# Two weight loads ahead of the second modulation group, convolution vectors moved up, and another order of passes in the first unit of a block

## The chip, the cores and the metric

The kernel runs on one core of a Trainium2 chip. The metric is device time of one execution in microseconds (us). Matmuls run on TensorE (PE in the profile; PEld is its weight load), elementwise work on VectorE (DVE), ScalarE (ACT) and GpSimd (POOL). Nearly all DMAs are issued by SyncE (SP), in the order of its program; a few small ones by ACT.

## What is computed

One layer of a decoder with T = 256 positions and D = 2048 channels, in float32:

```python
mod = silu(c) @ w_ada + b_ada            # shift, scale, gate for each of the two sub-layers
h   = rms_norm(x, g_mix_norm) * (1 + scale1) + shift1
p   = h @ w_in                           # columns: GLA k, q, v, gates; attention q, k, v
o   = concat(diff_attention(...), gla_chunked(...))
x   = x + gate1 * (o @ w_o)
h2  = rms_norm(x, g_ffn_norm) * (1 + scale2) + shift2
g, u = split(h2 @ w_up)
x   = x + gate2 * ((gelu(causal_dwconv(g, w_conv, b_conv)) * u) @ w_down)
out = rms_norm(x, g_final)
```

## The kernel before

**Units of weights.** Each weight matrix comes in units of 512 KB, two rows of 128 by 512 columns. `load_unit` (L110) has SP load a unit into `raw` (L120), lets ACT copy it into `wh`, rounded to the matmul's type (L123), and DVE subtract that from `raw` to give the low part `wl` (L124). The inputs (`hT`, `mixT`, `h2T`) are kept as a high and a low part too. A product is three matmuls: `wh` by high, `wh` by low, `wl` by high. `b_block` (L128, transposed output) and `a_block` (L159) run them. `wh` and `wl` have three buffers each, `raw` has six.

**The modulation vectors.** `w_ada` is multiplied in the background, by `ada_gen` (L219). Its loads `raw_a` (L240, 512 KB; L243 for the first group, in halves) use the same six buffers and the same queue of SP as the weights. The first of a group's 16 steps is an ACT multiplication into `acc` (L263), the other 15 are DVE multiply-adds (L265), each on top of the one before. Then PE sums over the partitions into `ps_mod` (L233), and DVE makes the columns `s` and `sh` of them (L278 to L281). Below, the 16 loads of the second group are called k0 to k15, and the first weight units w1, w2 and so on. How many background steps run per weight unit is a rate: `load_unit` adds `rate[0]` to a credit and takes one step for each whole credit. For the input projection `R_K` (L33) gives a rate for each of four input groups. `drain` runs a generator until a named step is done.

**Stages.** The input projection goes over four groups of 2, 4, 4 and 6 input tiles (loop at L747). In each group nine blocks of output columns are accumulated: the two lead blocks gk and gq half by half, then gv0, gv1, gg0, gg1, dq0, dk0, dv0. Group 0 needs the first modulation group, input group 1 the second. `norm_T` (L291) makes two input tiles: DVE scales by the row norm (L297), ACT applies `s` and `sh`. With gran = 1 (only the very first pair, of `hT` and of `h2T`) ACT writes the high part (L302) and the value `xv` itself (L304) tile by tile; otherwise the value (L304) and then both high parts at once (L306). DVE subtracts for the low part (L307).

Then come three later blocks, attention and GLA, and the output projection (`wo_part`): its first two column blocks in three parts of 4, 2 and 2 units, between them the second half of the attention in the background. After the last part of these stands the load of the convolution vectors (L845 to L851): four times a small DMA on ACT's queue into `cst` (three buffers), a transpose on PE and a copy on ACT. The up projection (`ps_h`) follows, in groups of 4, 4 and 8 input tiles, then the down projection.

**The order of the work.** The order of the instructions on an engine is set by a scheduler of the framework, which goes by priorities and a timeline of its own. An edit in one place can so move instructions in others. Each engine carries out its list in order, and a DMA is issued when SP's list comes to it and its buffer is free.

Of the kernel before, what the change touches and what calls it, by code (L numbers as in the profile page):

```python
# [7 lines left out]
F32 = mybir.dt.float32  # L8
# [3 lines left out]
AF = mybir.ActivationFunctionType  # L12
ALU = mybir.AluOpType
AX = mybir.AxisListType

P = 128
# [9 lines left out]
FT = D_FF // P  # L26
# [5 lines left out]

R_K, R_LATER, R_WO, R_SP, R_UP = (2.2, 1.15, 1.3, 1.0), 0.5, 0.8, 0.9, 0.27  # L33

# [12 lines left out]
def tile_decoder_layer(  # L47
# [46 lines left out]
    def drain(name):  # L94
        while any(n == name for n, _ in bg):
            step()
# [3 lines left out]
    def slot(tag, shape, dtype, name, bufs):  # L100
# [5 lines left out]
        return stage.tile(shape, dtype, tag=tag, name=name, bufs=bufs)  # L106

    def load_unit(view, kt, c0):
        credit[0] += rate[0]
        while credit[0] >= 1.0:  # L110
# [16 lines left out]
    def b_block(ps, view, c0, kts, xt, first, last, done=None, tail=0):  # L127
# [5 lines left out]
        for gi, group in enumerate(groups):  # L133
            ws = [(kt, *load_unit(view, kt, c0)) for kt in group]
            seq = [(kt, h, l, j, m) for kt, h, l in ws for j in range(2) for m in range(4)]
            if len(group) > 1:
                seq.sort(key=lambda x: x[4] // 2)
            for kt, h, l, j, m in seq:
                k = kt + j
                ms = slice(m * P, (m + 1) * P)  # L140
                for i, (w, xx) in enumerate(((h, 0), (h, 1), (l, 0))):
                    PE.matmul(  # L142
                        ps[:, m * T:(m + 1) * T], w[:, j, ms], xt[k][:, xx, :],
# [147 lines left out]
    def norm_T(tmp, rst, s_col, sh_col, k0, name, gran):  # L291
# [3 lines left out]
        for j in range(0, 2, gran):  # L295
# [3 lines left out]
            for i in range(j, j + gran):  # L299
                k = k0 + i  # L300
                if gran == 1:
                    A.activation(res[:, 0, i], val[:, i], AF.Identity, scale=s_col[:, k:k + 1],  # L302
                                 bias=sh_col[:, k:k + 1])
                A.activation(val[:, i], val[:, i], AF.Identity, scale=s_col[:, k:k + 1], bias=sh_col[:, k:k + 1])  # L304
            if gran > 1:
# [441 lines left out]
    for g, kts in enumerate(KG):  # L747
        last = g == len(KG) - 1
        drain(f"norm{kts[0]}")
        rate[0] = R_K[g]  # L750
        if g == 1:
# [57 lines left out]


    drain("gt1")
    KO = list(range(8, 16)) + list(range(0, 8))
# [26 lines left out]
    for a, b in ((0, 8), (8, 12), (12, 16)):  # L839
        if b == KT:  # L840
            fdrain()
        for nb in range(2):
            wo_part(nb, po[nb], a, b)

    for j in range(4):  # L845
        cst = t1.tile([FT, P], F32, tag="w2", name="cst", bufs=3)
        src = w_conv[0, j] if j < 3 else b_conv[0]
        nc.scalar.dma_start(out=cst, in_=src.rearrange("(r p) -> r p", p=P))
        ps = pss.tile([P, 512], F32, tag="ms", name="ps_cv")
        PE.transpose(ps[:, 0:FT], cst, ident[0:FT, 0:FT])  # L850
        A.activation(nconv[:, j], ps[:, 0:FT], AF.Copy)  # L851
    for nb in range(2, 4):
# [177 lines left out]
```

## Time and profile before

| | |
|---|---|
| median of 3 runs | 1301.42 us (1301.13 to 1303.23) |
| the profiled execution | 1301.91 us |
| its span, first to last instruction | 1300.2 us |
| PE busy | 1239.3 us |
| DVE busy | 888.1 us |
| ACT busy | 702.3 us |
| read from HBM | 311 MB |

All times in the rows below are microseconds from the start of the span of the one profiled execution. A row of a timeline gives start, duration and engine; `x2` marks merged instructions. An engine with a q behind its name (SPq, ACTq) is the issue of a DMA. The square bracket names the idle time before an instruction and the instruction whose end released it. The granted clock (PEclk) is a share of TensorE's full speed: 1.00 is 2.4 GHz, 0.50 is 1.2 GHz.

### The profile page before, as it was taken

The page shows a single profiled execution, that of the slowest core. Times are in us where ns is not written, and L with a number is a line of the kernel's source. Part 1 is how long each engine was busy: PE and PEld are TensorE (multiplying, and loading weights), DVE is VectorE, ACT ScalarE, POOL GpSimd, SP SyncE. Part 2 cuts the span into 40 slices and gives each one's busy share as a digit, 9 for nine tenths or more (in the row PEclk, how much of TensorE's full clock was granted, in tenths as well). Part 3 has the DMA queues.
Part 4 walks back from the last instruction along what each step waited for, and adds up shares of the span by engine and source line. Part 5 has one row for each costly group of instructions (what it writes and reads, how often), then busy time and mean ns, then how long its engine had stood idle before and what let it go on. Part 6 is the DMA issues. An engine that isn't in the chain of part 4 may idle for free.

```text
span 1300.2 us, 21317 instructions
## 1 busy us (share of the span) xinstructions
PE 1239.3 (95%) x8492; PEld 1145.4 (88%) x8492; DVE 888.1 (68%) x1137; ACT 702.3 (54%) x913; POOL 38.3 (3%) x79
## 2 busy tenths in 40 slices
PE   4799999999999989899999999999999999999996
PEld 3588898888888889799999999999999988888885
DVE  5788888877667666777765777766667554545454
ACT  5377676854544434566776665744444543434343
POOL 3044000000000000000000000000000000000000
PEclk9899999999999989899999999999999999999999
DMA  8999999875477657699897777766677855555562
GB/s 301 321 346 336 353 336 324 266 236 179 146 232 243 196 170 227 231 360 341 294 336 224 228 225 223 235 215 194 203 233 234 274 168 194 193 194 194 181 208 82
DMA packets 159827, 314.57 MB, mean 242 GB/s; under 512 B 12046, under 2 KB 20942, under 8 KB 159727
## 3 DMA queue, kind: packets, MB, share of 16 engines
q1 hardware_dynamic: 155328, 307.28, 72.4%
q10 hardware_dynamic: 4398, 5.93, 1.3%
q8 instruction: 66, 1.08, 0.3%
q14 instruction: 35, 0.28, 0.1%
HBM read 311.07 MB, written 2.10 MB: 241 GB/s over the span
## 4 chain that ended last, share of the span: by engine, by line
PE 82%; DMA 8%; DVE 5%; ACT 2%; issue 2%; DVEq 0%; ACTq 0%
PE ps_h L142 39%; PE ps_d L176 18%; PE ps_mm L142 8%; PE ps_mm L176 6%; DMA raw_a<-in_w_ada_dram 5%; PE ps_o L142 5%; DVE acc L265 2%; DMA raw<-in_w_in_dram 2%; DVE wl L124 1%; PE ps_mod L233 1%; PE ps_s L590 1%; ACT wh L123 1%; PE ps_a L533 1%; DMA xtok<-in_x_dram 1%; DMA dlam<-in_diff_lambda_dram 1%
## 5 line engine op out<-in xcount | busy, mean ns | idle before, releaser
L124 DVE TENSOR_TENSOR wl<-raw,wh 128x1024 fp32r<-128x1024 f32 x339 | 413.9, 1223 | 220.2 <-ACT wh L123 218.9
L123 ACT ACTIVATE wh<-raw 128x1024 fp32r<-128x1024 f32 x339 | 357.6, 1057 | 372.1 <-PE ps_d L176 123.0
L142 PE MATMUL ps_h<-h2T,wh 128*128 128x256 f32 x2304 | 419.2, 284 | 4.7 <-ACT h2T L302 3.5
L142 PEld LDWEIGHTS ps_h<-h2T,wh 128*128 128x128 f32 x2304 | 360.7, 193 | 5.4 <-ACT h2T L302 3.9
L142 PE MATMUL ps_h<-h2T,wl 128*128 128x256 f32 x1152 | 326.7, 284 | 0.0
L265 DVE SCALAR_TENSOR_TENSOR acc<-raw_a,cols,acc 128x1024 f32<-128x1024 f32 (+1 forms) x180 | 216.3, 1202 | 89.5 <-DMA raw_a<-in_w_ada_dram 88.0
L142 PEld LDWEIGHTS ps_h<-h2T,wl 128*128 128x128 f32 x1152 | 221.7, 192 | 0.0
L176 PE MATMUL ps_d<-wh,act 128*128 128x512 f32 x704 | 217.4, 389 | 0.8 <-DVE dx L988 0.8
L176 PEld LDWEIGHTS ps_d<-wh,act 128*128 128x128 f32 x704 | 132.1, 188 | 29.3 <-DVE dx L988 1.2
L142 PE MATMUL ps_mm<-hT,wh 128*128 128x256 f32 x768 | 144.7, 289 | 7.2 <-ACT wh L123 6.3
L176 PE MATMUL ps_d<-wl,act 128*128 128x512 f32 x352 | 137.8, 391 | 0.0
L142 PEld LDWEIGHTS ps_mm<-hT,wh 128*128 128x128 f32 x768 | 122.5, 196 | 10.3 <-ACT wh L123 6.9
L176 PE MATMUL ps_mm<-wh,hT 128*128 128x512 f32 x384 | 123.9, 398 | 6.1 <-ACT wh L123 5.2
L142 PE MATMUL ps_mm<-hT,wl 128*128 128x256 f32 x384 | 110.8, 290 | 1.5 <-DVE wl L124 1.5
L142 PE MATMUL ps_o<-mixT,wh 128*128 128x256 f32 x512 | 97.3, 291 | 4.5 <-ACT mixT L475 2.6
L142 PE MATMUL ps_h<-h2T,late 128*128 128x256 f32 x768 | 97.4, 283 | 0.0
L142 PEld LDWEIGHTS ps_h<-h2T,late 128*128 128x128 f32 x768 | 94.4, 192 | 0.0
L176 PEld LDWEIGHTS ps_mm<-wh,hT 128*128 128x128 f32 x384 | 73.4, 192 | 22.9 <-ACT wh L123 6.2
L142 PEld LDWEIGHTS ps_o<-mixT,wh 128*128 128x128 f32 x512 | 82.2, 197 | 6.6 <-ACT mixT L475 3.2
L176 PE MATMUL ps_mm<-wl,hT 128*128 128x512 f32 x192 | 77.5, 404 | 2.5 <-DVE wl L124 2.5
L176 PEld LDWEIGHTS ps_d<-wl,act 128*128 128x128 f32 x352 | 66.1, 188 | 13.9 <-issue 0.5
L142 PEld LDWEIGHTS ps_mm<-hT,wl 128*128 128x128 f32 x384 | 74.8, 195 | 2.5 <-DVE wl L124 2.0
(247 smaller groups left out, 1125.2 us busy)
## 6 DMA issues: line engine op xcount, KB each, us to landing
raw_a<-in_w_ada_dram SPq DMA_DIRECT2D x162, 512.0 KB, 5.0
raw<-in_w_up_dram SPq DMA_DIRECT2D x143, 512.0 KB, 4.6
raw<-in_w_in_dram SPq DMA_DIRECT2D x96, 512.0 KB, 5.5
raw<-in_w_down_dram SPq DMA_DIRECT2D x88, 512.0 KB, 4.2
late<-in_w_up_dram SPq DMA_DIRECT2D x33, 512.0 KB, 4.8
raw<-in_w_o_dram SPq DMA_DIRECT2D x32, 512.0 KB, 4.7
raw_a<-in_w_ada_dram SPq DMA_DIRECT2D x32, 256.0 KB, 5.4
late<-in_w_ada_dram SPq DMA_DIRECT2D x14, 512.0 KB, 5.2
```

Of the source, the lines that this page charges most:

```text
L123: A.activation(h, raw, AF.Copy)
L124: V.tensor_tensor(l, raw, h, op=ALU.subtract)
L142: PE.matmul(ps[:, m * T:(m + 1) * T], w[:, j, ms], xt[k][:, xx, :], start=(first and k == kts[0] and m % 2 == 0 and i == 0), stop=(last an ...
L176: PE.matmul(ps[:, tb * 512:(tb + 1) * 512], xt[k][:, xx, tsl], w[:, j, :], start=(first and k == kts[0] and i == 0), stop=(last and k == k ...
L233: PE.matmul(ps[:, i:i + 1], src[:, i * P:(i + 1) * P], col, start=(not began and i == 0), stop=False, skip_group_check=True)
L265: pin(V.scalar_tensor_tensor(acc, raw[:, j], col, acc, op0=ALU.mult, op1=ALU.add))
L533: PE.matmul(pv[:, i, tb], lhs, rhs, start=True, stop=True)
L590: PE.matmul(pv, q[rs, hb * T + tb * P:hb * T + (tb + 1) * P], k[rs, hb * T:hb * T + n], start=False, stop=(tb == 1), skip_group_check=True)
```

## The change

It has four parts. The first weight units of the two lead blocks are requested right after the inputs of group 0 are drained, before the rate is set and so without any background step between them (`pre`); they are handed out when `load_unit` is asked for them. To take up for the two units without credit, the rate of group 0 is 2.7 for 2.2. In `norm_T` with gran = 1, DVE writes the value instead of ACT. In `b_block`, the first unit of a block that has more than one unit runs `wh` by high and `wl` by high for all its columns first, and `wh` by low last. The loads of the convolution vectors move from the end of the first two column blocks of the output projection to before it.

```diff
-R_K, R_LATER, R_WO, R_SP, R_UP = (2.2, 1.15, 1.3, 1.0), 0.5, 0.8, 0.9, 0.27
+R_K, R_LATER, R_WO, R_SP, R_UP = (2.7, 1.15, 1.3, 1.0), 0.5, 0.8, 0.9, 0.27
...
+    pre = {}
+
     def load_unit(view, kt, c0):
+        if (kt, c0) in pre:
+            return pre.pop((kt, c0))
         credit[0] += rate[0]
...
-            seq = [(kt, h, l, j, m) for kt, h, l in ws for j in range(2) for m in range(4)]
+            seq = [(kt, h, l, j, m, (0, 1, 2)) for kt, h, l in ws for j in range(2) for m in range(4)]
             if len(group) > 1:
                 seq.sort(key=lambda x: x[4] // 2)
-            for kt, h, l, j, m in seq:
+            elif gi == 0 and len(groups) > 1:
+
+                seq = [x[:5] + (p,) for p in ((0, 2), (1,)) for x in seq]
+            for kt, h, l, j, m, passes in seq:
                 k = kt + j
                 ms = slice(m * P, (m + 1) * P)
                 for i, (w, xx) in enumerate(((h, 0), (h, 1), (l, 0))):
+                    if i not in passes:
+                        continue
...
                 if gran == 1:
                     A.activation(res[:, 0, i], val[:, i], AF.Identity, scale=s_col[:, k:k + 1],
                                  bias=sh_col[:, k:k + 1])
-                A.activation(val[:, i], val[:, i], AF.Identity, scale=s_col[:, k:k + 1], bias=sh_col[:, k:k + 1])
+                    V.tensor_scalar(val[:, i], val[:, i], s_col[:, k:k + 1], sh_col[:, k:k + 1],
+                                    op0=ALU.mult, op1=ALU.add)
+                else:
+                    A.activation(val[:, i], val[:, i], AF.Identity, scale=s_col[:, k:k + 1],
+                                 bias=sh_col[:, k:k + 1])
...
         drain(f"norm{kts[0]}")
+        if g == 0:
+            for bi in range(2):
+                pre[0, BLOCKS[bi][1]] = load_unit(w_in_v, 0, BLOCKS[bi][1])
         rate[0] = R_K[g]
...
+    for j in range(4):
+        cst = t1.tile([FT, P], F32, tag="w2", name="cst", bufs=3)
+        src = w_conv[0, j] if j < 3 else b_conv[0]
+        nc.scalar.dma_start(out=cst, in_=src.rearrange("(r p) -> r p", p=P))
+        ps = pss.tile([P, 512], F32, tag="ms", name="ps_cv")
+        PE.transpose(ps[:, 0:FT], cst, ident[0:FT, 0:FT])
+        A.activation(nconv[:, j], ps[:, 0:FT], AF.Copy)
...
     drain("gt1")
...
             wo_part(nb, po[nb], a, b)
-
-    for j in range(4):
-        cst = t1.tile([FT, P], F32, tag="w2", name="cst", bufs=3)
-        src = w_conv[0, j] if j < 3 else b_conv[0]
-        nc.scalar.dma_start(out=cst, in_=src.rearrange("(r p) -> r p", p=P))
-        ps = pss.tile([P, 512], F32, tag="ms", name="ps_cv")
-        PE.transpose(ps[:, 0:FT], cst, ident[0:FT, 0:FT])
-        A.activation(nconv[:, j], ps[:, 0:FT], AF.Copy)
     for nb in range(2, 4):
```

Lines after the change are higher by 4 to 17 than before: L120 is L124, L123 is L127, L240 is L249, L263 is L272, L142 is L151, L766 is L782.

SP's issues at the start, before the change. `raw_a<-in_w_ada_dram` of 512 columns are the loads k0 and on, `raw<-in_w_in_dram` the weights w1 and on:

```order
2 L243 DMA raw_a<-in_w_ada_dram 128x2x256 x16
3 L240 DMA raw_a<-in_w_ada_dram 128x2x512 x3
4 L120 DMA raw<-in_w_in_dram 128x2x512
5 L240 DMA raw_a<-in_w_ada_dram 128x2x512 x2
6 L120 DMA raw<-in_w_in_dram 128x2x512
7 L240 DMA raw_a<-in_w_ada_dram 128x2x512 x2
8 L120 DMA raw<-in_w_in_dram 128x2x512
9 L240 DMA raw_a<-in_w_ada_dram 128x2x512 x2
10 L120 DMA raw<-in_w_in_dram 128x2x512
11 L240 DMA raw_a<-in_w_ada_dram 128x2x512 x3
```

And with the change:

```order
2 L252 DMA raw_a<-in_w_ada_dram 128x2x256 x16
3 L249 DMA raw_a<-in_w_ada_dram 128x2x512
4 L124 DMA raw<-in_w_in_dram 128x2x512 x2
5 L249 DMA raw_a<-in_w_ada_dram 128x2x512 x2
6 L124 DMA raw<-in_w_in_dram 128x2x512
7 L249 DMA raw_a<-in_w_ada_dram 128x2x512 x3
8 L124 DMA raw<-in_w_in_dram 128x2x512
9 L249 DMA raw_a<-in_w_ada_dram 128x2x512 x3
10 L124 DMA raw<-in_w_in_dram 128x2x512
11 L249 DMA raw_a<-in_w_ada_dram 128x2x512 x2
```

Before, three modulation loads stood ahead of w1, and from then on one weight stood behind every two or three modulation loads. With the change k0 is followed by w1 and w2, w3 stands behind k2, and w4 behind k5.

ACT at the start, before the change (`hT` is the input's high part, `acc<-raw_a` the first step of the second modulation group, `pj_gk` and `pj_gq` the copies that close the lead blocks):

```order
28 L376 ACTIVATE lam_133<-lam_133 128x2
29 L302 ACTIVATE hT_287<-xv,sh_128,s_127 128x256 x2
30 L304 ACTIVATE xv<-xv,sh_128,s_127 128x256 x2
31 L263 ACTIVATE acc<-raw_a,cols 128x1024
32 L123 ACTIVATE wh<-raw 128x1024 x2
33 L766 ACTIVATE pj_gk<-ps_mm 128x1024
34 L123 ACTIVATE wh<-raw 128x1024
35 L766 ACTIVATE pj_gq<-ps_mm 128x1024
36 L123 ACTIVATE wh<-raw 128x1024
```

And with the change:

```order
28 L127 ACTIVATE wh<-raw 128x1024
29 L389 ACTIVATE lam_133<-lam_133 128x2
30 L127 ACTIVATE wh<-raw 128x1024
31 L311 ACTIVATE hT_287<-xv,sh_128,s_127 128x256 x2
32 L127 ACTIVATE wh<-raw 128x1024
33 L782 ACTIVATE pj_gk<-ps_mm 128x1024
34 L782 ACTIVATE pj_gq<-ps_mm 128x1024
35 L272 ACTIVATE acc<-raw_a,cols 128x1024
36 L782 ACTIVATE pj_gv_142<-ps_mm 128x1024
```

Before, `acc<-raw_a` stood ahead of the first `wh`. With the change it stands behind three `wh` and behind `pj_gk` and `pj_gq`. The two rows of L304 are gone from ACT.

PE at the first up-projection unit, before the change (`h2T_5250` is the first pair of inputs):

```order
2006 L142 MATMUL ps_h<-h2T_5250,wh 128x256 x3
2007 L142 MATMUL ps_h<-h2T_5250,wl 128x256
2008 L142 MATMUL ps_h<-h2T_5250,wh 128x256 x2
2009 L142 MATMUL ps_h<-h2T_5250,wl 128x256
2010 L142 MATMUL ps_h<-h2T_5250,wh 128x256 x2
```

And with the change, the end of the first unit's first passes and what follows:

```order
2050 L151 MATMUL ps_h<-h2T_5250,wl 128x256
2051 L151 MATMUL ps_h<-h2T_5250,wh 128x256
2052 L151 MATMUL ps_h<-h2T_5250,wl 128x256
2053 L151 MATMUL ps_h<-h2T_5250,wh 128x256 x5
2054 L151 MATMUL ps_h<-h2T_5250,wl 128x256
2055 L151 MATMUL ps_h<-h2T_5250,wh 128x256 x4
2056 L151 MATMUL ps_h<-h2T_5260,wh 128x256 x2
2057 L151 MATMUL ps_h<-h2T_5260,wl 128x256
```

Before, the three passes of a column stood together: `wh`, `wh`, `wl`. With the change the unit begins with `wh` and `wl` in turn, and its `wh` by low matmuls stand in the rows of x5 and x4, ahead of the second unit (`h2T_5260`).

## Rows read from the trace of the kernel before

**Rows 1.** The page: busy time, share of the span and number of instructions of each engine (part 1).

```profile
PE 1239.3 (95%) x8492; PEld 1145.4 (88%) x8492; DVE 888.1 (68%) x1137; ACT 702.3 (54%) x913; POOL 38.3 (3%) x79
```

**Rows 2.** The table by stretches: the stretch, its length, then the busy time of each engine in it (instructions in brackets), the granted clock of TensorE as a share of full speed, the busy share of the DMA engines, and what they moved.

```profile
20.00:40.00 20.00, 11.39 (x71) 10.39 (x70) 16.72 (x30) 9.40 (x15) 7.32 (x15) 0.74 0.88 288
...
520.00:540.00 20.00, 13.90 (x90) 12.71 (x89) 13.14 (x20) 10.79 (x17) 0.00 (x0) 0.83 0.47 144
...
30.00:34.00 4.00, 0.80 (x2) 0.50 (x2) 3.66 (x5) 2.68 (x4) 0.16 (x1) 0.50 0.64 192
...
40.00:77.00 37.00, 28.72 (x137) 23.56 (x136) 28.66 (x28) 20.19 (x24) 0.00 (x0) 0.86 1.00 347
77.00:220.00 143.00, 139.50 (x882) 123.89 (x883) 120.59 (x136) 100.53 (x114) 28.21 (x53) 1.00 0.99 341
```

**Rows 3.** The timeline around 455 us, where the last of the convolution vectors is loaded and transposed: start, duration, engine, line, operation, tiles, and in square brackets the idle time before and what ended it.

```profile
451.78 1.22 DVE L124 TENSOR_TENSOR wl<-raw,wh 128x1024 fp32r<-128x1024 f32 x1 [1.55 <-ACT wh L123]
...
454.27 0.37 SPq L240 DMA_DIRECT2D raw_a<-in_w_ada_dram  x1
...
455.23 0.30 ACTq L848 DMA_DIRECT2D cst<-in_b_conv_dram  x1
...
457.22 0.16 DVE L635 TENSOR_TENSOR ods<-ods,st 128x2 f32<-128x2 f32 x1
459.05 1.28 DVE L265 SCALAR_TENSOR_TENSOR acc<-raw_a,cols,acc 128x1024 f32<-128x1024 f32 x1 [1.67 <-DMA raw_a<-in_w_ada_dram]
...
459.26 0.30 PE L850 MATMUL ps_cv<-ident,cst 44*128 44x44 f32 x1 [3.48 <-DMA cst<-in_b_conv_dram]
...
460.25 0.60 DVE L637 SCALAR_TENSOR_TENSOR pj_dq<-ps_od,ods,gdiff 128x128 f32<-128x128 f32 x2
...
464.29 1.31 PE L142 MATMUL ps_o<-mixT,wh 128*128 128x256 f32 x3 [0.69 <-ACT mixT L475]
```

**Rows 4.** What SP's queue of DMA issues waited for from 18 to 80 us: total, times, longest.

```profile
SPq L240 <- DVE acc L265: 11.6, 13, 2.4
SPq L240 <- DVE wl L124: 10.3, 7, 2.8
```

**Rows 5.** The timeline of the start, 18 to 45 us, columns as before. A row with x2 or x3 is that many instructions merged, and its duration runs from the first to the end of the last.

```profile
18.51 3.31 SPq L240 DMA_DIRECT2D raw_a<-in_w_ada_dram  x3
...
19.90 0.38 ACTq L369 DMA_DIRECT2D dlam<-in_diff_lambda_dram  x1
...
23.10 0.37 SPq L120 DMA_DIRECT2D raw<-in_w_in_dram  x1
...
27.63 0.31 DVE L374 TENSOR_TENSOR dlam<-dlam 128x128 f32<-128x128 f32 x1 [0.82 <-DMA dlam<-in_diff_lambda_dram]
...
30.60 1.13 ACT L263 ACTIVATE acc<-raw_a,cols 128x1024 f32<-128x1024 f32 x1
...
31.76 0.37 SPq L120 DMA_DIRECT2D raw<-in_w_in_dram  x1
...
32.74 0.80 PE L142 MATMUL ps_mm<-hT,wh 128*128 128x256 f32 x2 [4.81 <-ACT wh L123]
...
34.26 0.58 PE L142 MATMUL ps_mm<-hT,wl 128*128 128x256 f32 x1 [0.73 <-DVE wl L124]
...
35.64 1.06 ACT L123 ACTIVATE wh<-raw 128x1024 fp32r<-128x1024 f32 x1 [2.95 <-DMA raw<-in_w_in_dram]
...
37.63 0.32 PE L142 MATMUL ps_mm<-hT,wl 128*128 128x256 f32 x1
...
39.18 0.37 SPq L120 DMA_DIRECT2D raw<-in_w_in_dram  x1
...
41.27 4.01 SPq L240 DMA_DIRECT2D raw_a<-in_w_ada_dram  x2
```

**Rows 6.** The timeline from 41 to 78 us, up to the first matmul of input group 1.

```profile
43.68 0.49 PE L176 MATMUL ps_mm<-wh,hT 128*128 128x512 f32 x1 [2.13 <-ACT wh L123]
...
64.78 1.28 DVE L265 SCALAR_TENSOR_TENSOR acc<-raw_a,cols,acc 128x1024 f32<-128x1024 f32 x1
...
71.54 0.16 DVE L281 SCALAR_TENSOR_TENSOR s<-s,cols 128x4 f32<-128x4 f32 x1
...
77.05 0.50 PE L142 MATMUL ps_mm<-hT,wh 128*128 128x256 f32 x2 [0.32 <-ACT ps_mm L761]
```

**Rows 7.** The timeline of the first up-projection units, 516 to 534 us.

```profile
526.61 0.80 PE L142 MATMUL ps_h<-h2T,wh 128*128 128x256 f32 x2 [3.48 <-ACT h2T L302]
528.05 0.59 ACT L302 ACTIVATE h2T<-xv,sh,s 128x256 fp32r<-128x256 f32 x1
...
528.65 0.58 PE L142 MATMUL ps_h<-h2T,wh 128*128 128x256 f32 x1 [1.25 <-DVE h2T L307]
...
529.19 1.03 DVE L307 TENSOR_TENSOR h2T<-xv,h2T 128x512 fp32r<-128x512 f32 x2 [0.59 <-ACT h2T L306]
529.25 0.63 PE L142 MATMUL ps_h<-h2T,wh 128*128 128x256 f32 x2
...
532.45 0.50 PE L142 MATMUL ps_h<-h2T,wh 128*128 128x256 f32 x2
...
532.90 0.40 PE L142 MATMUL ps_h<-h2T,wh 128*128 128x256 f32 x2
```

**Rows 8.** The groups by line with shapes kept apart, DVE: busy time, mean ns of one, idle time before.

```profile
L372 DVE TENSOR_SCALAR ggla<-ggla 128x256 f32<-128x256 f32 x1 | 0.5, 489 | 0.0
```

## The prediction

> **What bounds the kernel now.** I read the page's shares first: PE is busy for 1239.3 of 1300.2 us [rows 1]. So only the roughly 60 us in which PE does not work, and stretches at the lower clock, can be won or lost. The table by stretches says where some of those lie [rows 2]: from 77 to 220 us PE works 139.5 of 143 us, but from 20 to 77 us 40.1 of 57 (11.39 and 28.72) at a granted clock of 0.74 to 0.86, and from 520 to 540 us 13.90 of 20. The change touches both places, and a third, near 455 us, where the timeline shows PE waiting 3.48 us [rows 3].
>
> The start is not a PE matter. From 40 to 77 us the DMA share is 1.00 at 347 GB/s [rows 2], so one 512 KB load takes 524 KB / 347 = 1.5 us of the engines. Both streams, first weights and modulation rows, share SP's queue and six buffers. That the queue can still run dry is seen at 30 to 34 us: share 0.64 [rows 2]. SP's waits name the accumulations and low-part subtractions that free its buffers [rows 4].
>
> **The change, part by part. A, the start (18 to 77 us).** Now k0, k1 and k2, the first three loads of the second modulation group, take the slots from 18.51 to 21.8, the first weights w1 go out at 23.10 and w2 at 31.76 [rows 5]. With the change w1 and w2 take the second and third slot, near 20 and 21.4. A load issued at 19.90 (dlam) was used at 27.63 [rows 5]; with 8 us they land at 28 and 29.4. Then ACT makes wh1 to 29.1, wh2 to 30.6 and the input's high part to 31.1; DVE has two subtractions of 1.22, two val steps and the low part, done near 33.2. PE then runs steadily from 33.2 instead of 34.26 [rows 5]. At half clock for 3.4 us from there, as now (34.26 to 37.6), it does 16 of the lead blocks' 48 matmuls; 32 more at 0.12 end near 40.5 instead of 41.55, where PE's 2.13 us wait before 43.68 begins [rows 6]: **-1.0 us there**. The third block's weights are early too, so that wait goes.
>
> What is late next: the first multiplication of the second modulation group (acc k0, on ACT). It runs at 30.60 now [rows 5]. In the changed order it stands behind the copies of both lead blocks. The second copy ends 1.0 us after its block, near 41.5, and acc k0 near 42.5: 11 us late. Its buffer is what the fourth weight load waits for, so SP stands still before it, where that load now goes out at 39.18 [rows 5]. All 15 DVE accumulations start from acc k0. By 42.5 us the old order had issued 14 loads of 512 KB (the first at 18.51, the last in the row at 41.27 [rows 5]), the new one 10: four times 1.5 = 6.0 us of DMA time not used.
>
> From there I walk on: a load goes out when the last reader of its buffer is done and lands 1.5 us behind the one before it, an accumulation takes 1.28 [rows 6], a subtraction 1.22 [rows 3], wh 1.06 [rows 5]. w4 lands at 46.3; its subtraction ends at 48.3 and lets w5 go, which lands at 51.9; w6 lands at 56.4, w7 at 62.4, w8 at 66.9. k15, the last row of the group, is accumulated behind the subtraction of w8, by 70.5, against 66.06 now (64.78 + 1.28 [rows 6]). The ps_mod matmuls come one block later than before, behind the block that needs w8, and end near 73.7; s is ready at 74.2. From s to the first matmul of group 1 it took 71.70 to 77.05, 5.35 us [rows 6]. In the new order pj_gk's reload stands before that chain, so I take 4.9, which gives 79.1 for 77.05: **+2.1 us**. The credit rate changes little: 9 units at 2.2 are 19.8 steps, 7 at 2.7 are 18.9. Bounds: -1.0, all of the lead gain and nothing late; above, +6.0, all of the unused DMA time.
>
> After a pause in the queue, w2 landed 3.9 us after its issue (31.76 to the start of its wh at 35.64 [rows 5]); that is in the walk for w4. The Trainium skill (DMA: Bandwidth & Descriptors, "Anatomy of one DMA — SWDGE (gpsimd) path") has a fixed 2.0 us plus bytes over 436 GB/s, for loads issued by another path than this one. By that, an estimate of 3.2 us for 512 KB, w4 and all after it would be 0.7 us earlier, A +1.4 and the sum -2.2; no row here shows that path, and the row of w2 decides.
>
> **B, the convolution vectors (388 to 464 us).** The fourth of the small loads, b_conv, is issued at 455.23; its transpose, in front of ps_mod in PE's program, starts 4.0 us later and waits 3.48 us [rows 3]. Moved to the beginning of the output projection, the last two transposes stand behind 42 matmuls of two units, some 5 us at 0.12 each, which cover the 4 us of landing: 0 to 0.5 us of wait is left, and I take 0.3. At 455 us PE then goes into ps_mod at once. What ends last there is the accumulation on DVE that waits for its raw row, 459.05 now [rows 3]. In the new order it stands ahead of the small steps (ods), four of 0.16, and of pj_dq, 0.60. Its load goes out about 0.4 us behind a subtraction that ends at 453.0, so near 453.4 instead of 454.27, and lands 4.8 us later as now, at 458.2. Accumulation to 459.5, ods and pj_dq to 460.8, transposes and mixT to 462.2, for 464.29 [rows 3]: -2.1, plus 0.3 of the new wait: **-1.8 us**. Bounds: -3.5, the whole wait; +2, if the row takes 7.7 us, as dlam did at the start [rows 5], and the mixT copy near 445 us, now behind two softmax copies that it preceded, costs PE 1.3 more.
>
> **C, the first up-projection units (523 to 533 us).** PE starts at 526.61, does two matmuls, waits 1.25 us for the input's low part, which stands behind xv on ACT, and stays at half clock to 532.45 [rows 7]: a pair takes 0.63 instead of 0.40. In the new order the low-part matmuls of the first unit come last. The first 16 matmuls need only the first input's high part; at 0.213 us each (three in 529.25 to 529.89) they reach to 530.0, while the second input's high part is done at 528.64 and the last low part at 530.22 [rows 7]. So the wait goes and PE works without a gap from 526.6. I take it that the clock comes back as long after the first matmul without a gap as now (528.65 to 532.45, 3.8 us): 530.4, 2.05 us earlier, with two matmuls fewer done by then, 0.24: **-1.8 us**. Bounds: -1.0, the wait less a late second input, and -2.5. The val step, moved from ACT to DVE, takes 0.49 (a multiply of the same 128x256 shape [rows 8]), where a step of ACT took 0.59 [rows 7]. It lies beside the 16 matmuls; without that cover it would cost 0.49 twice.
>
> The other units whose passes are reordered have both parts in place before they start, and the count of matmuls is the same: 0.
>
> **Sum:** 2.1 - 1.8 - 1.8 = -1.5 us. The profiled execution took 1301.91 us, 1.7 more than its span and 0.5 above the median of 1301.42. Against the median: **1299.9 us**. A measurement of this kernel can tell about 0.2%, 2.6 us, from no change, so this forecast is no change, on the good side of it.
>
> **Rivals.**
> 1. *The modulation group is not late.* If loads land faster after the pause and DVE catches up, group 1 starts at about 76.0. For it: DVE works only 28.66 of 37 us from 40 to 77 [rows 2], and the lead blocks end early. Against it: acc k0's place. A is -1.0, the total -1.0 - 1.8 - 1.8 = -4.6: **1296.8 us**.
> 2. *The dry queue is never made good.* DMA is at 1.00 or 0.99 from 40 to 220 us [rows 2], so four loads not issued could come out whole, as 6.0 us; and PE, waiting longer for group 1, would start it at half clock, as it ran from 32.74 to 37.6 at the start [rows 5], which costs half of 4.9 us, 2.4. A is +8.4, the total +4.8: **1306.2 us**. It decides from a group 1 start after about 83 us. Against it: PE idles only 3.5 us from 77 to 220, so the queue has some slack there.
> 3. *The reordering does not act at C*, because DVE's or ACT's order holds PE as long. Total 2.1 - 1.8 = +0.3: **1301.7 us**. Against it: 16 matmuls that need one input's high part alone.
>
> **How the numbers follow.** Forecast 0.40, rival 1 0.35, rival 2 0.20, rival 3 0.05. Of the forecast 0.05 falls beyond 2.6 us faster, since B may give 3.5, and 0.03 beyond 2.6 slower; rival 1 gives 0.33 to faster and 0.02 to the same; rival 2 gives 0.19 to slower and 0.01 to the same; rival 3 is the same. Faster 0.38, same 0.40, slower 0.22. The range takes in rival 1 with a good us below it, to 1295.2, and half of rival 2, to 1306.0; beyond lie about 0.08 and 0.11. The forecast's own range, by B's and C's bounds, is 1297.5 to 1303.
>
> **What would show it.** PE's first steady matmul at 33.2; the acc on ACT at 41 to 42 and a DMA share well under 0.8 from 39 to 44 us; group 1's first matmul at 78 to 80; no PE wait above 0.5 at the last conv transpose, and PE back in the output projection 2 us sooner; no 1.25 us wait in the first up units and full clock 3.8 us after their first matmul. The prediction is wrong if group 1 starts before 77 or after 82, or if a wait appears behind 100 us that was not there.

## The result, and the profile after

The changed kernel takes 1320.4 us (median of 4, 1318.72 to 1321.36) beside 1302.33 us of the kernel before (median of 4): 18.1 us slower, ratio 1.0131 [1.0110, 1.0151]. The profiled execution took 1321.13 us, its span is 1319.4 us against 1300.2.

To see where the 19.2 us of span come in, I put marks along the program: the ACT copy that closes block gk of input group 1, the copies that close the last block (dv) of groups 2 and 3, the copy of the last of the later projection blocks, the first `ps_q` matmul behind the output projection, the first up-projection matmul and the end. Times in us from the span's start:

| | gk, group 1 | dv, group 2 | dv, group 3 | last projection block | first `ps_q` | first `ps_h` | end |
|---|---|---|---|---|---|---|---|
| before | 86.85 | 187.46 | 292.19 | 390.89 | 520.04 | 526.61 | 1300.2 |
| after | 97.51 | 199.85 | 306.00 | 408.59 | 541.32 | 547.90 | 1319.4 |
| later by | 10.7 | 12.4 | 13.8 | 17.7 | 21.3 | 21.3 | 19.2 |

Input projection and the stages up to 409 us: +17.7. Output projection (last projection block to `ps_q`): 129.2 before, 132.7 after, +3.5. From the first up matmul to the end: 773.6 before, 771.5 after, -2.1. Together they are 19.1 of the 19.2 us, and only the third place went as forecast.

PE is not the bound of what was lost: its busy time rose by 6.7 us, the span by 19.2 (page, part 1).

```profile
PE 1246.0 (94%) x8492; PEld 1150.2 (87%) x8492; DVE 889.3 (67%) x1141; ACT 701.3 (53%) x909; POOL 39.1 (3%) x79
```

The table by stretches of the changed kernel, in the columns of [rows 2]:

```profile
20.00:40.00 20.00, 13.12 (x83) 12.25 (x83) 13.52 (x30) 8.22 (x13) 9.21 (x15) 0.74 0.81 277
...
34.00:38.00 4.00, 4.00 (x28) 4.00 (x28) 1.03 (x1) 0.00 (x0) 0.00 (x0) 0.74 0.70 241
38.00:42.00 4.00, 4.00 (x28) 3.63 (x27) 0.00 (x0) 2.94 (x3) 0.00 (x0) 1.00 0.01 3
42.00:46.00 4.00, 0.79 (x4) 0.33 (x2) 3.75 (x3) 1.33 (x3) 0.00 (x0) 1.00 0.66 192
...
40.00:77.00 37.00, 26.87 (x119) 21.57 (x118) 28.97 (x26) 16.40 (x16) 0.00 (x0) 0.82 0.89 296
77.00:220.00 143.00, 132.86 (x835) 119.53 (x834) 115.70 (x132) 96.85 (x110) 27.51 (x53) 0.96 0.97 329
...
46.00:52.00 6.00, 4.59 (x10) 3.34 (x11) 5.10 (x5) 0.90 (x1) 0.00 (x0) 0.52 0.96 295
46.00:77.00 31.00, 24.08 (x106) 19.62 (x107) 25.22 (x24) 13.15 (x13) 0.00 (x0) 0.78 0.98 328
85.00:90.50 5.50, 5.17 (x22) 4.88 (x23) 5.50 (x9) 1.19 (x2) 5.29 (x9) 0.50 0.92 292
...
0.00:200.00 200.00, 161.16 (x902) 140.82 (x903) 149.34 (x197) 120.64 (x145) 39.12 (x79) 0.91 0.93 313
```

From 38 to 42 us the DMA engines stand all but still (share 0.01) while PE works without a gap. From 46 to 77 us their share is 0.98 again, which leaves no room there to make up for the pause. From 77 to 220 us PE does 132.9 us of work where it did 139.5 [rows 2], and from 85 to 90.5 us it has half the clock.

The timeline of the start, which answers to [rows 5]:

```profile
32.89 0.58 PE L151 MATMUL ps_mm<-hT,wh 128*128 128x256 f32 x1 [1.00 <-DVE hT L320]
40.08 1.03 ACT L782 ACTIVATE pj_gq<-ps_mm 128x1024 f32<-128x1024 f32 x1 [0.90 <-PE ps_mm L151]
41.00 1.15 ACT L272 ACTIVATE acc<-raw_a,cols 128x1024 f32<-128x1024 f32 x1
42.17 0.37 SPq L124 DMA_DIRECT2D raw<-in_w_in_dram  x1
42.18 3.93 DVE L274 SCALAR_TENSOR_TENSOR acc<-raw_a,cols,acc 128x1024 f32<-128x1024 f32 x3 [7.15 <-ACT acc L272]
45.84 1.06 ACT L127 ACTIVATE wh<-raw 128x1024 fp32r<-128x1024 f32 x1 [1.99 <-DMA raw<-in_w_in_dram]
46.95 0.80 PE L185 MATMUL ps_mm<-wh,hT 128*128 128x512 f32 x1 [4.16 <-ACT wh L127]
```

This is the predicted chain, link by link. acc k0 stands on ACT right behind the copy of gq and runs at 41.00 instead of 30.60; SP's fourth weight load goes out as it ends, and DVE, idle for 7.15 us, starts the accumulations. The queue's own waits (18 to 80 us; total, times, longest) name the same instruction, with the 6.7 us that [rows 4] doesn't have:

```profile
SPq L249 <- DVE acc L274: 12.5, 13, 2.4
SPq L249 <- DVE wl L128: 8.5, 5, 2.8
SPq L124 <- ACT acc L272: 6.7, 1, 6.7
```

The way from the modulation group to input group 1, for [rows 6]:

```profile
71.02 1.28 DVE L274 SCALAR_TENSOR_TENSOR acc<-raw_a,cols,acc 128x1024 f32<-128x1024 f32 x1
73.93 1.84 PE L242 MATMUL ps_mod<-ones,acc 128*128 128x1 f32 x16
76.69 0.16 DVE L290 SCALAR_TENSOR_TENSOR s<-s,cols 128x4 f32<-128x4 f32 x1
78.38 1.06 ACT L127 ACTIVATE wh<-raw 128x1024 fp32r<-128x1024 f32 x1 [2.17 <-DMA raw<-in_w_in_dram]
79.35 2.06 ACT L316 ACTIVATE xv<-xv,sh,s 128x256 f32<-128x256 f32 x4
83.16 1.14 ACT L319 ACTIVATE hT<-xv 128x512 fp32r<-128x512 f32 x2
83.83 0.58 PE L151 MATMUL ps_mm<-hT,wh 128*128 128x256 f32 x1 [5.19 <-ACT hT L319]
85.26 1.23 PE L151 MATMUL ps_mm<-hT,wh 128*128 128x256 f32 x2 [0.85 <-ACT ps_mm L777]
```

`s` is ready at 76.85 (its last step ends 0.16 us after 76.69), but ACT's list has a `wh` ahead of the `xv` steps, and that `wh` waits 2.17 us for its load. Group 1 starts at 83.83 and works on from 85.26, against 77.05 before.

The output projection, for [rows 3]:

```profile
466.94 1.15 ACT L272 ACTIVATE acc<-raw_a,cols 128x1024 f32<-128x1024 f32 x1 [4.65 <-DMA raw_a<-in_w_ada_dram]
468.78 0.59 ACT L488 ACTIVATE mixT<-ps_ot 128x512 fp32r<-128x512 f32 x1
469.43 0.51 PE L151 MATMUL ps_o<-mixT,wh 128*128 128x256 f32 x1 [4.28 <-ACT mixT L488]
482.83 0.68 PE L661 MATMUL ps_ot<-ident,pj_dq 128*128 128x128 f32 x2 [2.94 <-DVE pj_dq L650]
484.20 1.31 PE L151 MATMUL ps_o<-mixT,wh 128*128 128x256 f32 x3 [0.69 <-ACT mixT L488]
```

The 3.48 us wait of the transpose is gone. In its place PE waits 2.94 us for `pj_dq`, and ahead of it 4.28 us for a `mixT` that stands on ACT behind an accumulation that waits for its raw row. The same `mixT` cost 1.95 us before (PE's wait at 445.62 in the trace of before).

The up projection, for [rows 7] (the duration of the DVE step answers to [rows 8]):

```profile
547.90 0.48 PE L151 MATMUL ps_h<-h2T,wh 128*128 128x256 f32 x1 [3.48 <-ACT h2T L311]
548.07 0.41 DVE L313 TENSOR_SCALAR xv<-xv,s,sh 128x256 f32<-128x256 f32 x1
551.38 0.32 PE L151 MATMUL ps_h<-h2T,wh 128*128 128x256 f32 x1
551.54 0.28 PE L151 MATMUL ps_h<-h2T,wl 128*128 128x256 f32 x1
```

No wait follows the first matmul, and the short matmuls of the full clock begin 3.5 us after it.

### The profile page after: what moved, and what is told of

The parts are those of the page before. It is cut to its first block, busy times and chain, and to the rows that moved or that the text cites. A ratio compares the mean times of both kernels' runs of the same rounds, so it can differ in the third digit from the quotient of the medians.

```text
span 1319.4 us, 21309 instructions
## 1 busy us (share of the span) xinstructions
PE 1246.0 (94%) x8492; PEld 1150.2 (87%) x8492; DVE 889.3 (67%) x1141; ACT 701.3 (53%) x909; POOL 39.1 (3%) x79
## 4 chain that ended last, share of the span: by engine, by line
PE 75%; DMA 12%; DVE 8%; issue 3%; ACT 2%; DVEq 0%; ACTq 0%
PE ps_h L151 39%; PE ps_d L185 18%; DMA raw_a<-in_w_ada_dram 9%; PE ps_mm L151 7%; PE ps_mm L185 4%; PE ps_o L151 3%; DVE wl L128 3%; DVE acc L274 3%; DMA raw<-in_w_in_dram 2%; ACT wh L127 1%; PE ps_mod L242 1%; PE ps_s L603 1%; DMA xtok<-in_x_dram 1%; PE ps_a L546 0%; PE ps_low L732 0%
## 5 line engine op out<-in xcount | busy, mean ns | idle before, releaser
L127 ACT ACTIVATE wh<-raw 128x1024 fp32r<-128x1024 f32 x342 | 361.0, 1058 | 384.1 <-PE ps_d L185 123.0
L151 PE MATMUL ps_h<-h2T,wh 128*128 128x256 f32 x2304 | 420.0, 284 | 3.5 <-ACT h2T L311 3.5
L151 PEld LDWEIGHTS ps_h<-h2T,wh 128*128 128x128 f32 x2304 | 361.5, 193 | 3.9 <-ACT h2T L311 3.9
L151 PE MATMUL ps_h<-h2T,wl 128*128 128x256 f32 x1152 | 311.7, 284 | 0.0
L151 PEld LDWEIGHTS ps_h<-h2T,wl 128*128 128x128 f32 x1152 | 222.4, 193 | 0.0
L151 PE MATMUL ps_mm<-hT,wh 128*128 128x256 f32 x768 | 148.1, 292 | 11.5 <-ACT hT L319 5.2
L151 PEld LDWEIGHTS ps_mm<-hT,wh 128*128 128x128 f32 x768 | 124.6, 198 | 15.4 <-ACT hT L319 5.6
L185 PE MATMUL ps_mm<-wh,hT 128*128 128x512 f32 x384 | 126.7, 405 | 8.8 <-ACT wh L127 6.3
L151 PE MATMUL ps_mm<-hT,wl 128*128 128x256 f32 x384 | 108.9, 292 | 1.0 <-DVE wl L128 1.0
L151 PE MATMUL ps_o<-mixT,wh 128*128 128x256 f32 x512 | 99.6, 295 | 6.9 <-ACT mixT L488 5.0
L151 PE MATMUL ps_h<-h2T,late 128*128 128x256 f32 x768 | 97.7, 284 | 0.0
L151 PEld LDWEIGHTS ps_h<-h2T,late 128*128 128x128 f32 x768 | 94.5, 192 | 0.0
L151 PEld LDWEIGHTS ps_o<-mixT,wh 128*128 128x128 f32 x512 | 83.9, 200 | 9.4 <-ACT mixT L488 5.5
L151 PEld LDWEIGHTS ps_mm<-hT,wl 128*128 128x128 f32 x384 | 75.8, 198 | 1.8 <-DVE wl L128 1.4
```

Of the source, the lines that this page charges most:

```text
L127: A.activation(h, raw, AF.Copy)
L151: PE.matmul(ps[:, m * T:(m + 1) * T], w[:, j, ms], xt[k][:, xx, :], start=(first and k == kts[0] and m % 2 == 0 and i == 0), stop=(last an ...
L185: PE.matmul(ps[:, tb * 512:(tb + 1) * 512], xt[k][:, xx, tsl], w[:, j, :], start=(first and k == kts[0] and i == 0), stop=(last and k == k ...
```

## Experiments

The runs are called e1 to e16, and each result below begins with its name. The text in front of it is what was expected before it ran. Each ratio is against the kernel before on the same chip, with its 95% interval; runs on different chips are compared by their ratios. A shift is the difference at a mark of the table above, in one profiled execution. How much of a shift is scatter is seen in e7 and e14: up to the last projection block their instructions on SP, ACT, DVE and PE are those of the kernel before, in the same order, and still they are 0.8 and 1.4 us later at group 2's dv, 1.8 and 3.8 at the last projection block. The theory: the late acc k0 starves the DMA queue, the DMA engines bound the kernel up to some 200 us, and what they did not move there comes out whole. The rivals: the rate 2.7 does it; the reordered passes or the conv vectors do it.

**Which part of the change.** The loads ahead with rate 2.7, alone in the kernel before:

```diff
-R_K, R_LATER, R_WO, R_SP, R_UP = (2.2, 1.15, 1.3, 1.0), 0.5, 0.8, 0.9, 0.27
+R_K, R_LATER, R_WO, R_SP, R_UP = (2.7, 1.15, 1.3, 1.0), 0.5, 0.8, 0.9, 0.27
...
+        if (kt, c0) in pre:
+            return pre.pop((kt, c0))
...
+        if g == 0:
+            for bi in range(2):
+                pre[0, BLOCKS[bi][1]] = load_unit(w_in_v, 0, BLOCKS[bi][1])
         rate[0] = R_K[g]
```

> Only the two weight loads ahead and the rate 2.7, on the kernel before. Theory 1 (the first step of the second modulation group, acc k0, is late and everything lost comes from it): all of the loss is here, 1319 to 1325 us, acc k0 at 41 us, group 1 first matmul at 83 to 86 us. Theory 3 (the moved convolution vectors and the new pass order lose some 10 us in the output projection): 1310 to 1313 us, with the shift of 8 to 11 us at group 1 and no more behind it.

e1: 1319.34 us, 1.0120 [1.0094, 1.0146]: nearly the whole loss. Shifts +8.8, +13.4, +12.7, +17.0 at the first four marks.

The change without that part (no `pre`, rate 2.2):

> The change without the loads ahead and with the rate 2.2. Theory 1: no loss, 1296 to 1300 us, from the pass order at the up projection (-2) and the convolution vectors (-1 to -3.5). Theory 3: 1308 to 1312 us.

e2: 1303.1 us, 1.0003 [0.9991, 1.0015]. The loss is the loads ahead with their rate. The rest gives nothing, where B and C should have given 3.6 us; neither theory had expected that.

**Is it acc k0's place?** The change, with one background step ahead of the two loads:

```diff
         if g == 0:
+            step()
             for bi in range(2):
```

> The whole change, with one background step taken before the two weight loads, so that acc k0 stands ahead of the first wh on ACT as before the change; the two weights still go out before k2. Theory 1: the DMA pause at 38 to 42 us goes, group 1 starts at 74 to 78 us, total 1293 to 1299 us. Theory 2 (weights that go out earlier push the modulation rows back whatever ACT does): group 1 at 82 to 86 us, total 1312 to 1320 us.

e3: acc k0 at 30.34; 1305.62 us, 1.0024 [1.0011, 1.0037]. The shift at group 2's dv is +2.0 where it was +12.4. One step that moves the head of the chain takes back four fifths of the loss. The total is above the 1293 to 1299 us of theory 1, since B and C give nothing here either. But the step also moves the loads, so I took the place by itself: the first ACT step no longer kept in program order, so that the scheduler may put it forward, and the loads in the order of the change.

```diff
-                    pin(A.activation(acc, raw[:, j], AF.Copy, scale=col))
+                    A.activation(acc, raw[:, j], AF.Copy, scale=col)
```

> The whole change; only the first step of a modulation group (acc k0, on ACT) is no longer kept in program order, so that on ACT it stands ahead of the first wh again. SP's first 20 issues have the same order as in the change: k0, w1, w2, k1, k2, w3, k3 to k5, w4. Theory 1 (acc k0 behind the lead blocks' copies is what dries the queue): w4 is issued before 38 us, no DMA share below 0.5 in 38 to 42 us, group 1 at 74 to 78 us, total 1297 to 1303 us. Theory 2 (the weights ahead push the modulation rows back in the queue, whatever ACT does): group 1 at 82 us or later, 1312 us or more.

e9: 1309.23 us, 1.0057 [1.0037, 1.0077]. In its timeline (ACT, SP, PE) acc k0 runs at 24.86 and the fourth weight load goes out at 32.53, and group 1 starts 3.8 us earlier than in the kernel before. SP's list is that of the change up to 670 us; on ACT and DVE, other steps moved too, from 32 us on:

```profile
24.86 1.15 ACT L272 ACTIVATE acc<-raw_a,cols 128x1024 f32<-128x1024 f32 x1 [1.33 <-DMA raw_a<-in_w_ada_dram]
32.53 0.37 SPq L124 DMA_DIRECT2D raw<-in_w_in_dram  x1
73.24 0.51 PE L151 MATMUL ps_mm<-hT,wh 128*128 128x256 f32 x2 [2.02 <-ACT ps_mm L777]
```

Of the +12.4 at group 2's dv, +1.1 is left, so with the loads in the same order it is acc k0's place that decides at the start. Yet the early start is given back by then, and the total is above the 1297 to 1303 us expected: the shift grows to +4.5 at the last projection block and +7.4 at `ps_q`. The table by stretches:

```profile
0.00:40.00 40.00, 21.21 (x114) 19.23 (x115) 25.32 (x61) 20.81 (x35) 12.39 (x26) 0.87 0.94 317
0.00:200.00 200.00, 167.97 (x1002) 149.23 (x1003) 157.84 (x208) 127.45 (x154) 44.11 (x79) 0.95 0.98 333
```

The kernel before moved 289 GB/s up to 40 us and 334 up to 200. The early start moved more at first (317), but over 200 us no more bytes (333).

**Is the rate to blame?** The loads ahead with rate 2.2, and the rate 2.7 without them:

> The two loads ahead with the rate left at 2.2. Theory 1 (that the two lead units take no background step, so acc k0 comes behind them, is the cause; the rate is not): as slow as with 2.7, 1316 to 1323 us. Rival (the rate decides, the lost credits being made up or not): with fewer steps in group 0, 2 us or more slower than that, or, if the crowding at 2.7 was the trouble, 1308 us or less.

e6: 1310.69 us, 1.0055 [1.0034, 1.0077]; acc k0 at 42.89. Neither expectation held: the lateness without the higher rate costs some two fifths of the loss.

> Only the rate of group 0 is 2.7, on the kernel before; the lead units take their steps. Open: the run with rate 2.2 lost 7 us where the same with 2.7 lost 16, with the same start. If the rate by itself puts more steps into group 0 than fit and costs later: 1306 to 1311 us. If it only matters where the lead units take none: within 2 us of before.

e12: 1312.66 us, 1.0084 [1.0059, 1.0109]. acc k0 is in place (32.09), and it is still slow, by a little more than was expected: at 2.7 three modulation loads stand ahead of each of the next two weight loads, which go out at 34.59 and 39.57 (31.76 [rows 5] and 35.43 in the kernel before). SP's rows of this run, and its table by stretches:

```profile
26.63 6.99 SPq L240 DMA_DIRECT2D raw_a<-in_w_ada_dram  x3
34.59 0.37 SPq L120 DMA_DIRECT2D raw<-in_w_in_dram  x1
35.73 2.89 SPq L240 DMA_DIRECT2D raw_a<-in_w_ada_dram  x3
39.57 0.37 SPq L120 DMA_DIRECT2D raw<-in_w_in_dram  x1
```

```profile
0.00:200.00 200.00, 161.70 (x923) 141.19 (x924) 152.58 (x202) 124.05 (x152) 38.55 (x79) 0.93 0.95 321
```

So the rate is a cause of its own, by the same sign: fewer bytes moved. With the early acc k0 of e9 and the up projection's pass order alone, at 2.7 and at 2.2 (`view is w_up_v` added to the condition in `b_block`):

> As the run before, with the new pass order in the up projection alone. If the output projection's new order costs 1 to 1.5 us: 1 us faster than the run before, 1296 to 1302 us; if not, the same as it within 0.5 us.

e10: 1305.11 us, 1.0016 [1.0000, 1.0032]: 4.1 us faster than e9 on the same chip, more than either case had it.

> Loads ahead, acc k0 early, pass order in the up projection alone, convolution vectors moved, and the rate 2.2: differs from the run with 1305.1 us in the rate alone. If the rate costs 3 us or more at the later blocks: 1299 to 1302 us. If not: 1304 to 1306 us.

e13: 1310.47 us, 1.0058 [1.0035, 1.0081], outside both expectations. With two lead units that pay nothing, 2.2 takes the steps later: k15 is accumulated at 68.31, in e10 at 63.26. No rate is the better one in all cases: with the loads ahead and acc k0 late it is 2.2 (e6 against e1), with the loads ahead and acc k0 early 2.7 (e10 against e13), and without the loads ahead 2.2 again (the kernel before against e12).

**Are the DMA engines the bound?** The kernel before with five further loads of 512 KB by SP, into tiles that are overwritten before anything reads them, right after the inputs of group 0 (L749):

```diff
         drain(f"norm{kts[0]}")
+        if g == 0:
+            for n, kt in (("gg0", 0), ("gg1", 2), ("dq0", 4), ("dk0", 6), ("dv0", 8)):
+                nc.sync.dma_start(out=pj[n].rearrange("p (a b) -> p a b", a=2), in_=w_up_v[:, kt:kt + 2, 0:512])
```

> The kernel before with five more loads of 512 KB at the head of SP's first weights, into tiles that are written later anyway; nobody reads them. Every other instruction keeps its place. Theory 1 (up to 200 us the DMA engines are what bounds this kernel, so unused or wasted DMA time comes out whole): five times 1.5 us, +7 to +9 us, 1309 to 1312 us. Rival (the chain of accumulations or ACT bounds the start and DMA has slack): 0 to +3 us, 1302 to 1306 us.

e5: 1307.04 us, 1.0031 [1.0017, 1.0045]: +4.0, half of what their 7.6 us of DMA time would cost.

```profile
0.00:40.00 40.00, 17.96 (x78) 16.02 (x79) 20.38 (x55) 18.27 (x33) 9.92 (x26) 0.81 0.96 334
0.00:200.00 200.00, 167.17 (x979) 146.68 (x980) 155.18 (x204) 127.82 (x155) 38.31 (x79) 0.94 0.98 340
```

The first 40 us had room: they moved 334 GB/s instead of 289, 1.8 of the extra 2.6 MB. The other 0.8 MB stand for 2.4 us at 345 GB/s, beside a shift of 3.1 at group 2's dv. So before 40 us the engines have room. That they are the bound from there on fits, but is not shown by this run: acc k0 is already 2.6 us late in it (33.23 for 30.60), group 1's gk 3.0, and the shift hardly grows from there to group 2's dv. A late chain of accumulations would look the same.

**The second and third place, each alone.** Conv vectors moved; pass order of all first units and the value on DVE; pass order in the up projection only and the value on DVE:

> Only the convolution vectors moved. If the 3.48 us wait at 459 us is what bounds that place: 1300 to 1301.5 us against 1303 of before, -1.5 to -3. If a row of the background accumulation on DVE bounds it, whose wait takes the place of the one removed: 1302.5 to 1304 us, no change, with a wait of 1 us or more of ps_ot or ps_o for pj_dq or mixT near 460 us.

e7: 1301.84 us, 0.9993 [0.9982, 1.0003], between the two ranges.

> Only the new pass order in the first unit and the value step on DVE, on the kernel before. Theory 1: -1.5 to -3 us, 1298.5 to 1300.5 us, from the start of the up projection alone. Theory 3: the order of passes costs time in the output projection, 1304 us or more.

e4: 1303.01 us, 1.0003 [0.9987, 1.0019]: in neither of the two ranges.

> The new pass order in the up projection alone, and the value step on DVE; the output projection keeps its order. If the pass order gains 1.7 to 2.3 us at the start of the up projection and costs something in the output projection: 1300.5 to 1301.5 us, -1.5 to -2.5. If not: within 1 us of before.

e8: 1301.52 us, 0.9988 [0.9975, 1.0002]. None of the three can be told from the kernel before by its time. In the profiles the third place is plain. From the first `ps_h` to the end, the seven kernels without the new order in the up projection (before, e1, e5, e6, e7, e12, e14) take 773.2 to 774.2 us, the eleven with it (after, e2, e3, e4, e8 to e11, e13, e15, e16) 771.3 to 772.1. The second place is less so. The output projection takes 126.4 us in e7 for 129.2, but 127.5 and 127.0 in e5 and e6, where the vectors did not move. By the waits of PE in it (those over 0.2 us): 9.5 us before, 7.6 in e7, which is the 1.9 that was forecast, and 12.1 in the change.

Conv vectors and the up projection's order together, without the loads ahead:

> The convolution vectors moved and the new pass order in the up projection alone, on the kernel before: no loads ahead, rate 2.2. Sum of two earlier runs, -1.2 and -1.5 us: 1300 to 1301 us where before is at 1303. If the two don't add up because the same row of the accumulation ends both places: 1301.5 to 1303 us.

e11: 1299.97 us, 0.9981 [0.9967, 0.9994]: faster than the kernel before by about 2.5 us, clear of its interval. Against e2 it leaves out the pass order of the other first units, and only that: the "0" of the prediction. To find which units, the order in the output projection alone (with the conv vectors), and everywhere but there:

> The convolution vectors moved and the new pass order in the output projection alone; nothing else. Differs from the run with 1301.8 us in that order alone. If that order costs time there: 1303.5 to 1306 us, with the stretch from the end of the projections to the first ps_q 2 to 4 us longer than in that run. If the cost seen in three pairs came from elsewhere: 1301 to 1302.5 us.

e14: 1302.04 us, 1.0001 [0.9985, 1.0017].

> Convolution vectors moved, value step on DVE, and the new pass order everywhere but in the output projection: differs from the fast kernel (ratio 0.998) in the pass order of dq and dk in the projection, and from the run without the loads ahead (ratio 1.000) in the output projection's. The output projection's order alone has cost nothing measurable. If dq and dk's order costs the 3 us: ratio 0.9995 to 1.001. If it takes both orders together: ratio 0.997 to 0.999.

e15: 1305.62 us, 1.0014 [0.9997, 1.0031]. e15 and e11, whose intervals lie apart, differ only in the order of passes in the projection blocks with transposed output (dq and dk), so it is these; the ratios put it at 4.3 us. The cost comes out later: e15's output projection takes 133.0 us, e14's 126.9 and e11's 126.6, in profiled executions that lie 8.2 us apart for e15 and e11. e15's waits of PE there, and ahead of the second what DVE does:

```profile
398.41 0.39 PE L147 MATMUL ps_o<-mixT,wl 128*128 128x256 f32 x1 [1.42 <-DVE wl L124]
400.91 1.28 DVE L270 SCALAR_TENSOR_TENSOR acc<-raw_a,cols,acc 128x1024 f32<-128x1024 f32 x1 [2.55 <-DMA raw_a<-in_w_ada_dram]
402.11 1.22 DVE L124 TENSOR_TENSOR wl<-raw,wh 128x1024 fp32r<-128x1024 f32 x1
403.38 0.39 PE L147 MATMUL ps_o<-mixT,wl 128*128 128x256 f32 x1 [1.42 <-DVE wl L124]
...
453.44 0.38 PE L147 MATMUL ps_o<-mixT,wh 128*128 128x256 f32 x1 [2.79 <-ACT mixT L484]
```

and e11's wait for the same `mixT`:

```profile
447.24 0.39 PE L147 MATMUL ps_o<-mixT,wh 128*128 128x256 f32 x1 [0.89 <-ACT mixT L484]
```

The two waits for `wl` and the longer one for `mixT` are 4.7 of the 6.4 us between them. Nothing was edited there: the scheduler's lists came out differently. SP's list is the same in both runs, DVE's differs from 303 us on and ACT's from 308. At the second wait e15 has an accumulation ahead of the `wl`, and it waits 2.55 us for its raw row; in e11 that `wl` stands ahead of that accumulation.

**A version that beats both.** e11 with the first accumulation free to go ahead, as in e9:

> The fast kernel (vectors moved, pass order in the up projection), and acc k0 free of the program order. SP's order is that of before, so little can move: if the DMA engines bound the kernel up to 200 us, within 1 us of the fast kernel, ratio 0.997 to 0.9995; if an earlier acc k0 lets the queue fill earlier and that lasts, 2 to 3 us faster than it, ratio 0.996.

e16: 1299.0 us, 0.9968 [0.9953, 0.9984], the lowest ratio of all and faster than the kernel before; from e11 it cannot be told apart, their intervals overlap. acc k0 at 25.58, shift -2.2 at group 1's gk, -0.9 at group 2's dv, 0.2 at the last projection block: of the early start nothing clear of the scatter is left. The output projection takes 125.7 us, the rest from the first `ps_h` 771.8.

## Why the prediction was wrong

**A, the start: the mechanism held, the price did not.** The term that failed is A's +2.1. It was taken at group 1's first matmul and held to be all; there it was already 6.8, at the copy of gk 10.7, and +17.7 at the last projection block, far above the upper bound of +6.0. e1 has 17.0 of that with this part alone. Step by step:

| step | predicted | measured |
|---|---|---|
| PE steady | 33.2 | 32.89 |
| acc k0 | 42.5 | 41.00 |
| w4 lands | 46.3 | 45.84 (its `wh`) |
| k15 accumulated | 70.5 | 72.30 |
| s ready | 74.2 | 76.85 |
| from s to group 1's first matmul | 4.9 | 7.0 |
| group 1's first matmul | 79.1 | 83.83 |

w4 took 3.67 us from issue to `wh`. By the page of the Trainium skill that the prediction quotes (DMA: Bandwidth & Descriptors, "Anatomy of one DMA — SWDGE (gpsimd) path"), whose fit is for loads issued by GpSimd and not by SP, it would be an estimate of 3.2. By w2's row it would be 3.9, and this row lies between the two.

Three steps failed. *First*, "In the new order pj_gk's reload stands before that chain, so I take 4.9". The reload does stand there, but so does a `wh`, and it waits 2.17 us for its load: 2.5 us pass between `s` and the first `xv`, where it was 0.04 before. In e1 `xv` starts right behind `s` (77.47 after 77.43), but two `wh` and a copy stand between it and the reload, and it is 6.9 us all the same. The order shown ahead of the prediction reached only to the lead blocks. The other 2.7 us of the 4.7 came before: `s` itself was late.

*Second*, the walk ended at group 1's first matmul, as if everything behind it would move by the same. The 10.7 at the copy of gk are 6.8 at that matmul, 1.4 until PE goes on at 85.26, and, as an estimate from 5.17 us of work at half clock from 85 to 90.5 us, 2.6 for the clock. Nor was it made up later, which the bytes moved show. Over the first 200 us the changed kernel moves 313 GB/s for 334, which is 4.2 MB, or 12.2 us at 345 GB/s; group 2's dv is 12.4 us later. The same sum for e12 (321) gives 7.5 beside 10.8, for e6 (314) 11.6 beside 10.2, for e13 (322) 7.0 beside 4.8, for e3 (331) 1.7 beside 2.0, for e9 (333) 0.6 beside 1.1, for e1 (313) 12.2 beside 13.4: the size is right, single runs are off by up to 3.3 us. Up to 77 us the loss is 2.1 MB (277 for 288 GB/s from 20 to 40 us, 296 for 347 from 40 to 77), or 6.1 us, just the four loads that the prediction set as its upper bound. They were only the first half: from 77 to 220 us the queue moved 329 GB/s for 341, another 1.7 MB or 5.0 us, behind the late `s` and the half clock of group 1's start. That the sum of bytes fits does not by itself say what held them back: a kernel that is late for any reason has moved fewer bytes by 200 us. For the DMA engines as the reason speak their share of 0.98 from 46 to 77 us and of 0.97 from 77 to 220, and that loads put in cost time (e5); a test that leaves no other reason was not run.

*Third*, "The credit rate changes little", by 19.8 steps against 18.9, so that it was put at nothing. The count was right and does not decide; which loads stand ahead of which weight does. e12 has the rate alone, and 1.0084.

What matters in the change is the background steps, moved away from between the two units: with one of them put back ahead of the loads (e3) the start is as before. acc k0 falls back because the early modulation groups are kept in program order (`pin`): without that it runs at 24.86 (e9).

**Rival 2, at 0.20, is what happened**, by its own sign: a group 1 start "after about 83 us", here 83.83, and half clock behind it. Its price, +8.4, was two thirds of what group 2's dv shows and less than half of the 17.7.

**B, the conv vectors: as forecast alone as far as the waits show, lost in company.** Predicted -1.8. e7, e11, e14 and e16 shorten the output projection by 2.8, 2.6, 2.3 and 3.5; e5 and e6 shorten it by 1.6 and 2.1 without it, so this is not all B. In the changed kernel it is 3.5 longer, outside the bounds of -3.5 and +2. The loads ahead by themselves are enough to lose it: e10 and e13, with the old order in the projections, take 130.0 and 130.8 us. The bound that the prediction named above, a raw row that comes late and the `mixT` copy behind other work on ACT, is close to what the trace shows at 466.94, only larger: there `mixT` stands behind an accumulation that waits 4.65 us for its row, which costs PE 2.3 us more than before, and `pj_dq` costs 2.94.

**C, the up projection: right.** Predicted -1.8; -2.1 in the change, and -1.5 to -2.3 in every kernel that has it. The wait is gone, the full clock came 3.5 us after the first matmul (3.8 predicted).

**The other units whose passes are reordered: the 0 was wrong.** By the ratios it costs 4.1 us between e10 and e9, 2.9 between e11 and e2, and 2.0 between e8 and e4, the last within the noise. e14 and e15 put it to the dq and dk blocks of the projections. PE's own work is the same there, as predicted; the scheduler's lists are not. The waits for `wl` and `mixT` are shown, and for the second `wl` the accumulation ahead of it; why the scheduler orders ACT and DVE otherwise after such a change was not settled.

**Open:** why e1, which starts like e6 and moves as many bytes by 200 us, loses 8.5 us more by the ratios; in the profiles it is 3.2 us later at group 2's dv, 4.5 at the last projection block and 7.2 at `ps_q`. And why the changed kernel goes from 12.4 to 17.7: from 187 to 410 us it has waits of PE for `wl` in projection blocks, 4.4 us in all, that the kernel before doesn't have; what delays these was not traced.

## What to carry to other kernels

A load moved ahead takes no time from anything by itself; look at what it pushes back, and follow that to the buffer which the DMA queue waits for. Where the DMA engines are busy to the end of a stretch, do the sum in bytes moved by that end, not in the delay of the next matmul alone: the early starts here that moved no more bytes were given back, and the pause of the queue, 6.1 us of loads by 77 us, came out as 10.7 at gk. An edit that costs nothing where it stands can still move a scheduler's list elsewhere, so time it by itself before it is joined to others that gain.

## What the runs showed of the hardware

After a pause of the DMA queue one 512 KB load took 3.67 us to its first reader, where in the stream the loads follow one another at 1.5 us. DVE's multiply-and-add with two columns on 128x256 took 0.41 us, less than the 0.49 of the multiply in [rows 8] and the 0.59 of the ACT step that it replaced. After 5.19 us of waiting PE ran group 1's start at half clock (0.50 from 85 to 90.5 us), and after 4.16 us of waiting it had 0.52 from 46 to 52 us.
